# A gated encoder layer: the first column pair's ramp products made plainly, one matmul at a time

## The chip, the cores and the metric

The kernel runs on one core of a Trainium2 chip. The metric is device time in microseconds of one execution. The core's engines appear in the profile as PE (TensorE matmuls) and PEld (TensorE weight loads), DVE (VectorE), ACT (ScalarE), POOL (GpSimd) and SP (SyncE, which issues nearly all loads and stores).

## The reference

One encoder layer on x of 1024 tokens by 2048 channels, all in float32:

```python
mod = jax.nn.silu(c) @ w_ada + b_ada                    # w_ada is 2048 x 6144
shift, scale, gate = jnp.split(mod, 3, axis=-1)
h = rmsnorm(x, pre_g) * (1.0 + scale[:, None]) + shift[:, None]
proj = h @ w_in                                          # 2048 x 4608
q, k, v, gate_a, u, gate_p = jnp.split(proj, SPLIT_POINTS, axis=-1)
y_a = windowed_gqa(q, k, v, rel_table, sink) * jax.nn.silu(gate_a)
y_p = multiscale_pool(u, w_pool_grp, pool_scale) * jax.nn.silu(gate_p)
g = jax.nn.sigmoid(h @ w_merge + b_merge)                # 2048 x 4096
g_a, g_p = jnp.split(g, N_BRANCHES, axis=-1)
merged = g_a * (y_a @ w_br_attn) + g_p * (y_p @ w_br_pool)
o = merged @ w_out
return x + gate[:, None] * rmsnorm(o, post_g)
```

## The kernel before

**The big product.** h times the 8704 columns of w_in and w_merge is worked in 34 column pairs of 256 columns, in the order of the list `ORDER`. Its contraction over 2048 channels is done in two passes of 1024 channels, that is, eight row tiles of 128 (`PART[0]`, then `PART[1]`); the sums of the first pass go to DRAM and are added in the second. A pass of a pair is one call of `strassen`: seven products in place of eight blocks. The operands on h's side are seven combinations, `MOVING = ("B11", "T3", "T2", "B21", "T4", "T1", "B22")`, each made once for a pair of row tiles, "tile j" below (j = 0 to 3 for the first pass, tile j being channel tiles 2j and 2j+1), of 128 x 512 elements. The operands on the weights' side are made anew for every column pair.

Each float32 operand is split by `split` (L93) into a high part (ScalarE copies to fp32r, L95) and a low part (VectorE subtracts, L96). A product is three matmuls for each tile j: high by high, high by low, low by high (L235). With two tiles a pair takes 7 x 2 x 3 = 42 matmuls, with four 84.

**The ramp.** No product can start before x is normalised, turned (transposed by TensorE against a scaled identity, `turn_rows`, L407), and modulated by scale and shift, and these come from silu(c) times w_ada, 256 columns per tile j. `modulation(j, ...)` is four steps of four w_ada tiles each: a TensorE matmul per w_ada tile (`GEMV`, L455; two records each in the trace), then in the last step a copy of the sums (L462), sums over columns (`PM`, L426), and two small VectorE operations that write `modc` (L430, L433). `fill(j)` then modulates the four xT blocks of tile j in place (two on ScalarE at L502, two on VectorE at L504), forms the combinations, and splits all seven (`put`).

To start before all of w_ada is there, the first `RAMP = 4` column pairs are done in halves: first with tiles 0 and 1 alone, results to `ramp_d`, then with tiles 2 and 3, adding those parts (`ramp_gen`). Modulations 2 and 3 stand as side steps between the products of the first half (`side`, called from `run`), `fill(2)` and `fill(3)` after it. The first pair's first three weights are prepared early (`ahead=True`). `run` leaves each pair's last product to the next pair (`flush`). After the ramp, 22 pairs carry one list of side work in the first pass, and the remaining pairs carry another (the second half of x and its modulation, 38 steps).

**Buffers and order.** All instructions are written by a Python program and put in order, for each engine, by a planner that takes the program's order as priority and may move a ready instruction ahead of one that isn't ready. `keep` pins an instruction to its place in the program among those that are pinned. 56 shared buffers of 256 KB (`slot`) hold xT, rows of x, w_ada tiles and in the end the 4 x 14 operands; a load waits until its buffer is free. `claim(j)` reserves tile j's 14. PSUM has eight banks under the tags `mm` (2), `sc` (2), `at` (2), `z0` and `z1` (`SEEDED`). `OPEN` is one matmul in each seeded bank ahead of its first accumulation (L578).

Of the kernel before, what the change touches and what calls it, by code (L numbers as in the profile page):

```python
# [3 lines left out]

# [8 lines left out]
F32 = mybir.dt.float32  # L13
F32R = mybir.dt.float32r
AF = mybir.ActivationFunctionType
ALU = mybir.AluOpType
# [26 lines left out]
def encoder_layer(ctx: ExitStack, tc: tile.TileContext, x, c, table, w_ada, b_ada, pre_g,  # L43
# [32 lines left out]
    def uid(s):  # L76
        cnt[0] += 1
        return f"{s}_{cnt[0]}"
# [42 lines left out]

    NIN = 4608
    JP = KT // 4
    RAMP = 4
    bias_d = dram.tile([NH, P * LINE], F32, name="bias_d")
    line_d = dram.tile([NH, LINE], F32, name="line_d")
    part_d = dram.tile([NIN + 2 * D, S], F32, name="part_d")
# [49 lines left out]
            fill()  # L177
        fills.extend([fill] * len(groups))

    def load_raws(w, n0, rows, js):  # L180

        raws = []
        nj = len(js)
        joint = wp.tile([P, 2, nj, 256], F32, tag="raw", name=uid("raw"), bufs=4) if nj < 4 else None
        for kh in range(2):
            r = joint[:, kh] if nj < 4 else wp.tile([P, nj, 256], F32, tag="raw", name=uid("raw"), bufs=4)
            load(r, rows(w, js, kh)[:, :, n0:n0 + 256])
            raws.append(r)
        return raws

# [16 lines left out]
            load(parts[blk], part(blk))  # L207
        return parts

    def strassen(w, n0, rows, js, op, ev, finish, part=None, raws=None, ahead=False):  # L210

# [55 lines left out]
        if ahead:  # L267
            wts = iter(list(wts))
            yield
# [88 lines left out]

    scz = xa2.tile([P, KT, 32], F32, name="scz")
    nc.vector.memset(scz, 0.0)  # L360
    pr = bank("at")
    nc.tensor.transpose(pr[:, 0:104], rows, ident[0:104, 0:104])
    nc.scalar.activation(sc, pr[:, 0:16], AF.Silu)
    nc.scalar.activation(scz[:, :, 0], pr[:, 0:16], AF.Silu)
    nc.scalar.activation(cols, pr[:, 0:104], AF.Copy)

    PART = [range(8), range(8, 16)]
    xT = {}
# [15 lines left out]
    def norm_rows(si):  # L384
        ssq = ep.tile([P, 8], F32, tag="ssq", name=f"ssq{si}", bufs=4)
        for q in range(4):
            xt = xts[si, q]
            if q < 2:
                junk = bank("sc", "junk")
                nc.scalar.activation(junk, xt, AF.Square, accum_out=ssq[:, q:q + 1])  # L390
# [5 lines left out]
        nc.scalar.activation(ssq[:, 5:6], ssq[:, 4:5], AF.Sqrt, bias=eps_t, scale=1.0 / D)  # L396
# [4 lines left out]
    def turn_rows(s):  # L401

        for q in range(2):
            banks = [bank(t, "XT1") for t in ("mm", "mm", *SEEDED)]
            for m in range(4):
                for j in range(4):
                    nc.tensor.matmul(banks[j][:, m * P:(m + 1) * P], xts[4 * s + m, q][:, j * P:(j + 1) * P],  # L407
                                     turn[4 * s + m], start=True, stop=True)
            for j in range(4):
                if j % 2 == 0:  # L410
                    nc.vector.tensor_copy(xT[q * 4 + j, s], banks[j])
                else:
                    nc.scalar.activation(xT[q * 4 + j, s], banks[j], AF.Copy)

    def ada_tile(j, q):
        at = xa.tile([P, 2, 4, P], F32, tag="xa", name=uid("ada"))
        for kk in range(2):
            r0 = (2 * q + kk) * P
            load(at[:, kk].rearrange("p (g h) n -> p g (h n)", g=2), w_ada[r0:r0 + P, 0:2 * D].rearrange("p (g n) -> p g n", g=2)
                 [:, :, j * 256:(j + 1) * 256])  # L420
        return at

    def sum_columns(acc):
# [5 lines left out]
    def mod_columns(j, pm):  # L429
        tc.keep_in_program_order(nc.vector.tensor_tensor(  # L430
            modc[:, :, :, j], pm[:, 0:4].rearrange("p (g h) -> p g h", g=2),
            cols[:, 16:48].rearrange("p (g k) -> p g k", g=2)[:, :, 2 * j:2 * j + 2], ALU.add))
        nc.vector.scalar_tensor_tensor(modc[:, 1, :, j], modc[:, 1, :, j], 1.0,  # L433
                                       cols[:, 48 + 2 * j:50 + 2 * j], op0=ALU.add, op1=ALU.mult)

    def ada_slots(j):
        tiles = []
        for kc in range(KT):
            tiles.append(slot("ada", F32, (P, 4, P)))
            load(tiles[kc].rearrange("p (g h) n -> p g (h n)", g=2),  # L440
                 w_ada[kc * P:(kc + 1) * P, 0:2 * D].rearrange("p (g n) -> p g n", g=2)
                 [:, :, j * 256:(j + 1) * 256])
        return tiles

    def modulation(j, tile_of, pin=False):

        st_ = {}

        def step(q):
            if q == 0:  # L450
                st_["pv"] = bank("at", "GEMV")
            pv = st_["pv"]
            for kc in range(4 * q, 4 * q + 4):
                g = kc % 4 * 32
                ins = nc.tensor.matmul(pv[g:g + 32, :], scz[:, kc, :], tile_of(kc), start=kc < 4,  # L455
                                       stop=kc >= 12, tile_position=(0, g))
                if pin:
                    tc.keep_in_program_order(ins)
            if q == 3:
                acc = xa2.tile([P, 4, P], F32, tag="acc", name=uid("acc"), bufs=2)  # L460
                tc.keep_in_program_order(
                    nc.scalar.activation(acc, pv.rearrange("p (g n) -> p g n", g=4), AF.Copy))  # L462
                mod_columns(j, sum_columns(acc))

        return [lambda q=q: step(q) for q in range(4)]

    def weigh(acc, t, kc):

# [27 lines left out]

        return [(lambda q=q: load_(q), lambda q=q: sum_(q)) for q in range(8)], lambda: mod_columns(j, st_["pm"])

    def modulate(eng, t, k):
        j, kh = k // 2, k % 2  # L500
        if eng is nc.scalar:
            eng.activation(t, t, AF.Identity, scale=modc[:, 1, kh, j:j + 1], bias=modc[:, 0, kh, j:j + 1])  # L502
        else:
            eng.tensor_scalar(t, t, modc[:, 1, kh, j:j + 1], modc[:, 0, kh, j:j + 1],  # L504
                              op0=ALU.mult, op1=ALU.add)

    op = new_op()
    PAIRS = (NIN + 2 * D) // 256
# [10 lines left out]
    def fill(j):  # L519
# [13 lines left out]
        for name, src in (("T3", b11), ("T4", b21), ("T1", b12), ("B22", b22)):  # L533
            put(op, name, j, src)

    def ramp_gen(jj, i, parts, **kw):
# [6 lines left out]
    raws = [load_raws(*weight_of(ORDER[0]), rows_in_turn(0), [0, 1])]  # L543
    ada = [ada_slots(0), ada_slots(1)]
    claim(0)
    ada.append(ada_slots(2))
    claim(1)
    raws += [load_raws(*weight_of(ORDER[i]), rows_in_turn(0), [0, 1]) for i in range(1, RAMP)]
    ada3 = [ada_tile(3, q) for q in range(5)]

    def tile3(kc):
        if kc // 2 == len(ada3):
            ada3.append(ada_tile(3, kc // 2))
        return ada3[kc // 2][:, kc % 2]

    side = deque(modulation(2, ada[2].__getitem__, True))
    for n, step in zip((6, 9, 12, 15), modulation(3, tile3, True)):
        side.extend([lambda: None] * (n - len(side)) + [step])
    for s in range(2):
        for si in range(4 * s, 4 * s + 4):  # L560
            norm_rows(si)
        turn_rows(s)
    early.close()
    nc.vector.tensor_scalar(nsink_t, sink_t, -1.0, None, op0=ALU.mult)
    for step in modulation(0, ada[0].__getitem__):
        step()
    fill(0)
    gen = ramp_gen(0, 0, None, ahead=True)
    next(gen)
    for step in modulation(1, ada[1].__getitem__):  # L570
        step()
    fill(1)

    for tag in SEEDED:
        hi = op["B11"][0][0]
        nc.tensor.matmul(bank(tag, "OPEN"), hi[:, 0:P], hi, start=True, stop=True)  # L578
# [885 lines left out]
```

## Time and profile before

| what | value |
|---|---|
| median of 3 runs | 2123.35 us (2121.32 to 2123.44) |
| profiled execution, its own time | 2122.46 us |
| its span | 2120.7 us, 28959 instructions |
| mean granted TensorE clock | 0.998 |
| HBM traffic | 340.41 MB read, 125.85 MB written |

The page gives busy time by engine, the span in 40 slices, and the chain of waits that ended last. A row of the timeline has start, duration, engine, line, operation, result and operands, the count, and in brackets the idle time before it and what ended it. A row of the windows has the stretch, its length, the busy time of PE, PEld, DVE, ACT and POOL with the number of instructions, the granted TensorE clock (1.00 is full), the DMA share and GB/s; when asked for one line only, the engines that this line runs on. A row of the chain has start, duration and what the chain ran through. Matmuls are pipelined, so the duration of one is longer than its spacing from the next.

### The profile page before, as it was taken

To read this page: it belongs to the slowest core of one execution; us is meant where nothing else is said; L and a number is where in the kernel's file an instruction comes from. 1 tells how busy PE (TensorE), PEld (TensorE's weight loads), DVE (VectorE), ACT (ScalarE), POOL (GpSimd) and SP (SyncE) were. 2 spreads that over 40 slices of the span, in tenths; PEclk is the share of its full clock that TensorE was granted. 3 is DMA by queue.
4 is the path that set the end of the run, shared out by engine and by line. 5 is a ranking of instruction groups with operands and counts; after the bars stand their busy time and mean duration, and the time that the engine had idled before them with its cause. 6 is when DMAs were issued, how large, how long until landed. Compare 5 with 4: busy or idle time off the path is not lost.

```text
span 2120.7 us, 28959 instructions
## 1 busy us (share of the span) xinstructions
PE 2089.0 (99%) x9567; PEld 1715.1 (81%) x9567; DVE 1538.7 (73%) x2754; ACT 1109.5 (52%) x2102; POOL 20.4 (1%) x90
## 2 busy tenths in 40 slices
PE   6999999999999999999999999999999999999998
PEld 4588888888888888888888888888788788888886
DVE  5786667777547676677777678856957977889667
ACT  5654444444474544666665544333645644767654
POOL 0000000000000000000000000000000000000000
PEclk9999999999999999999999999999999999999999
DMA  9886566899676356544645477676754556686996
GB/s 330 271 269 216 187 208 219 307 310 316 223 228 210 120 176 204 174 157 159 196 149 162 154 236 235 206 221 195 237 173 160 187 194 198 218 311 216 296 342 221
DMA packets 301718, 466.10 MB, mean 220 GB/s; under 512 B 23882, under 2 KB 144866, under 8 KB 301568
## 3 DMA queue, kind: packets, MB, share of 16 engines
q1 hardware_dynamic: 298192, 455.72, 65.9%
q0 software_dynamic: 3040, 8.48, 1.1%
q8 instruction: 75, 1.23, 0.2%
q14 instruction: 75, 0.61, 0.1%
q10 hardware_dynamic: 336, 0.06, 0.0%
HBM read 340.41 MB, written 125.85 MB: 220 GB/s over the span
## 4 chain that ended last, share of the span: by engine, by line
PE 90%; DVE 5%; DMA 3%; issue 1%; ACT 1%; SPq 0%; ACTq 0%; DVEq 0%
PE Z L235 30%; PE X L235 20%; PE V L235 20%; PE Z L1194 2%; PE Z L1195 2%; PE Z L1196 2%; PE V L1196 1%; PE X L1196 1%; PE X L1195 1%; PE V L1195 1%; PE V L1194 1%; PE X L1194 1%; PE GEMV L455 1%; DMA raw<-in_w_merge_dram 1%; DVE wlo L96 1%; PE PT L905 1%
## 5 line engine op out<-in xcount | busy, mean ns | idle before, releaser
L95 ACT ACTIVATE whi<-raw 128x512 fp32r<-128x512 f32 (+1 forms) x528 | 321.8, 610 | 526.1 <-PE Z L235 260.4
L96 DVE TENSOR_TENSOR wlo<-raw,whi 128x512 fp32r<-128x512 f32 (+1 forms) x528 | 347.0, 661 | 166.7 <-PE Z L235 129.8
L96 DVE TENSOR_TENSOR wlo<-wr,whi 128x512 fp32r<-128x512 f32 x224 | 151.0, 688 | 55.9 <-ACT whi L95 49.8
L95 ACT ACTIVATE whi<-wr 128x512 fp32r<-128x512 f32 x224 | 138.8, 629 | 89.7 <-DVE wlo L96 37.2
L102 DVE TENSOR_TENSOR raw<-raw,raw 128x512 f32<-128x512 f32 x80 | 55.2, 690 | 105.0 <-DMA raw<-in_w_merge_dram 77.2
L235 PE MATMUL V<-T3h,whi 128*128 128x512 f32 x336 | 92.0, 393 | 0.6 <-DVE u L102 0.6
L235 PE MATMUL X<-B11h,whi 128*128 128x512 f32 x336 | 92.0, 392 | 0.0
L95 ACT ACTIVATE whi<-ws 128x512 fp32r<-128x512 f32 (+1 forms) x88 | 53.7, 611 | 73.0 <-PE X L235 67.7
L235 PE MATMUL V<-T4l,whi 128*128 128x512 f32 x336 | 91.2, 390 | 0.7 <-DVE T4l L96 0.6
L235 PE MATMUL Z<-T1h,whi 128*128 128x512 f32 x336 | 91.6, 391 | 0.0
L235 PE MATMUL Z<-T2h,whi 128*128 128x512 f32 x336 | 91.5, 392 | 0.1
L235 PE MATMUL Z<-B22h,whi 128*128 128x512 f32 x336 | 91.5, 392 | 0.0
L235 PE MATMUL Z<-T2h,wlo 128*128 128x512 f32 x336 | 90.8, 390 | 0.5 <-DVE wlo L96 0.5
L235 PE MATMUL X<-B21h,whi 128*128 128x512 f32 x336 | 91.2, 391 | 0.0
L235 PE MATMUL V<-T4h,whi 128*128 128x512 f32 x336 | 91.2, 391 | 0.0
L235 PE MATMUL Z<-T1l,whi 128*128 128x512 f32 x336 | 91.0, 390 | 0.1
L235 PE MATMUL X<-B11l,whi 128*128 128x512 f32 x336 | 90.9, 390 | 0.0
L235 PE MATMUL X<-B11h,wlo 128*128 128x512 f32 x336 | 90.7, 390 | 0.0
L235 PE MATMUL Z<-B22l,whi 128*128 128x512 f32 x336 | 90.7, 390 | 0.0
L235 PE MATMUL V<-T3l,whi 128*128 128x512 f32 x336 | 90.7, 390 | 0.0
L235 PE MATMUL Z<-T1h,wlo 128*128 128x512 f32 x336 | 90.6, 390 | 0.0
L235 PE MATMUL X<-B21l,whi 128*128 128x512 f32 x336 | 90.6, 389 | 0.0
(315 smaller groups left out, 4819.3 us busy)
## 6 DMA issues: line engine op xcount, KB each, us to landing
part<-part_d SPq DMA_DIRECT2D x136, 256.0 KB, 4.8
ada<-in_w_ada_dram SPq DMA_DIRECT2D x128, 256.0 KB, 5.3
raw<-in_w_in_dram SPq DMA_DIRECT2D x64, 512.0 KB, 4.1
raw<-in_w_merge_dram SPq DMA_DIRECT2D x64, 512.0 KB, 5.8
wr<-ws_dS SPq DMA_DIRECT2D x64, 512.0 KB, 5.2
wr<-in_w_out_dram SPq DMA_DIRECT2D x48, 512.0 KB, 5.4
proj_d<-part SPq DMA_DIRECT2D x68, 256.0 KB, 2.2
sw<-in_w_out_dram SPq DMA_DIRECT2D x64, 256.0 KB, 5.7
```

What stands on the lines that cost most here:

```text
L95: ins = (nc.scalar.activation(hi, src, AF.Copy), nc.vector.tensor_tensor(lo, src, f32(hi), ALU.subtract))
L96: nc.vector.tensor_tensor(lo, src, f32(hi), ALU.subtract))
L102: return (eng or nc.vector).tensor_tensor(o, a, b, ALU.add)
L235: nc.tensor.matmul(ps, w_[:, i], op[mov][j][m_], start=fresh and i == 0 and n == 0, stop=i == nj - 1 and n == 2, skip_group_check=True)
L455: ins = nc.tensor.matmul(pv[g:g + 32, :], scz[:, kc, :], tile_of(kc), start=kc < 4, stop=kc >= 12, tile_position=(0, g))
L905: nc.tensor.transpose(pt[:, i * P:(i + 1) * P], p[:, i * P:(i + 1) * P], ident)
L1194: nc.tensor.matmul(pb, hi, w[0], start=first, stop=False, skip_group_check=True)
L1195: nc.tensor.matmul(pb, lo, w[0], start=False, stop=False, skip_group_check=True)
L1196: nc.tensor.matmul(pb, hi, w[1], start=False, stop=last, skip_group_check=True)
```

## The change

- The first column pair's first half is no longer a `strassen` call. `plain_block` makes each of its four result blocks from 12 matmuls (48 for 42), `piece` by `piece`, all pinned, in `mm` banks for the left half of tokens and `sc` banks for the right. Its weights are the raw ones, split (`first_weights(j)`).
- The pieces of tile 0 stand between the `GEMV` matmuls of modulation 1, tile 1's after it. The last round of x transposes (`turn_round`) stands between those of modulation 0, in two half rounds.
- `fill(0)` and `fill(1)` become `fill_blocks`, in which ScalarE writes the high part of each modulated block directly while VectorE modulates in place and subtracts, and `fill_sums` for the combinations. The upper right block gets operands of its own (`B12h`, `B12l`) in a pool that is freed after the plain products.
- The second ramp pair's first two weights are split ahead and given to it (`given`).
- `RAMP` is 5. Loads of w_ada for group 3 go partly to shared buffers (six of 16), and the raw weight loads are spread: pair 0's after group 0, pairs 1 and 2 after group 1, pairs 3 and 4 after group 3. Raw loads and the `ada_tile` loads are pinned.
- Modulation 2's first step stands before the last plain block; its other steps and those of modulation 3 stand at every second side slot of the next two pairs.
- Small vectors' activations follow the first row tile's squares.

```diff
-    RAMP = 4
+    RAMP = 5
...
-            yield prep(a11)
-            s3 = wp.tile([P, nj, P], F32, tag="ws", name=uid("ws"))
-            sub(s3, a11, a21)
-            yield prep(s3)
+            yield from given
+            if not given:
+                yield prep(a11)
+                s3 = wp.tile([P, nj, P], F32, tag="ws", name=uid("ws"))
+                sub(s3, a11, a21)
+                yield prep(s3)
...
+    def fill_blocks(j, between=None):
+        (b11, b12), (b21, b22) = ((xT[k, 0], xT[k, 1]) for k in (2 * j, 2 * j + 1))
+        right = tuple(bp.tile([P, 512], F32R, tag=t, name=uid(t)) for t in ("B12h", "B12l"))
+        for n, ((hi, lo), t, k) in enumerate(((op["B11"][j], b11, 2 * j), (op["B21"][j], b21, 2 * j + 1),
+                                              (right, b12, 2 * j), (op["B22"][j], b22, 2 * j + 1))):
+            keep(modulate(nc.scalar, t, k, hi))
+            keep(modulate(nc.vector, t, k))
+            if n < 3:
+                keep(sub(lo, t, f32(hi)))
+            if between:
+                between(n)
+        return right
+
+    def fill_sums(j):
+        (b11, b12), (b21, b22) = ((xT[k, 0], xT[k, 1]) for k in (2 * j, 2 * j + 1))
+        keep(sub(b12, b12, b11))
+        t2 = rp.tile([P, 512], F32, tag="tf", name=uid("tf"), bufs=2)
+        keep(sub(t2, b22, b12))
+        keep(sub(b11, t2, b11))
+        hi, lo = op["B22"][j]
+        keep(sub(lo, b22, f32(hi)))
+        split(*op["T3"][j], b11, True)
+        split(*op["T2"][j], t2, True)
+        keep(sub(b21, b21, t2))
+        for name, src in (("T4", b21), ("T1", b12)):
+            split(*op[name][j], src, True)
...
+    ada = [ada_slots(0)]
+    fetch_raws(0)
+    ada.append(ada_slots(1))
+    fetch_raws(1)
+    fetch_raws(2)
     claim(0)
     ada.append(ada_slots(2))
     claim(1)
     ada3 = [ada_tile(3, q) for q in range(5)]
+    ada3 = [at[:, kk] for at in ada3 for kk in range(2)] + ada_slots(3, range(10, KT))
+    for i in range(3, RAMP):
+        fetch_raws(i)
+    group2 = deque(modulation(2, ada[2].__getitem__, True))
+    side = deque()
+    for n, step in zip((1, 3, 5, 7, 9, 11, 13), list(group2)[1:] + modulation(3, ada3.__getitem__, True)):
+        side.extend([lambda: None] * (n - len(side)) + [step])
...
+    def plain_block(blk, j):
+        nt, s = int(blk[0]) - 1, int(blk[1]) - 1
+        def piece(n):
+            if j == n == 0:
+                opened[blk] = bank("mm" if s == 0 else "sc", "PB")
+            whi, wlo = (w[:, :, nt * P:(nt + 1) * P] for w in weights0[j])
+            mov = (op["B11"][j], op["B21"][j]) if s == 0 else (right_top[j], op["B22"][j])
+            kh, w, m = ((0, whi, 0), (0, wlo, 0), (1, whi, 0), (1, wlo, 0), (0, whi, 1), (1, whi, 1))[n]
+            keep(nc.tensor.matmul(opened[blk], w[:, kh], mov[kh][m], start=j == n == 0,
+                                  stop=j == 1 and n == 5, skip_group_check=True))
+            if j == 1 and n == 5:
+                t = ev.tile([P, 512], F32, tag="ev", name=uid("c"))
+                keep(nc.scalar.activation(t, opened[blk], AF.Copy))
+                store(block(ramp_d[0], 0)(blk), t)
+        return [partial(piece, n) for n in range(6)]
...
+    s0, s1, s2, s3 = modulation(0, ada[0].__getitem__, True)
+    turns, put_by = turn_round(1, 1, (0, 1))
+    s0()
+    s1()
+    take(turns, 8)
+    put_by()
+    turns, put_by = turn_round(1, 1, (2, 3))
+    s2()
...
+    s3(while_copied, lambda: take(turns, 1))
+    take(turns, 3)
     early.close()
...
+    right_top.append(fill_blocks(0))
+    put_by()
+    first_weights(1)
+    s0, s1, s2, s3 = modulation(1, ada[1].__getitem__, True)
+    pieces = deque(p for blk in ("11", "21", "12", "22") for p in plain_block(blk, 0))
+    take(pieces, 6)
+    s0()
+    take(pieces, 6)
+    s1()
+    fill_sums(0)
+    s2(None, lambda: take(pieces, 1))
...
+    s3(while_copied, lambda: take(pieces, 1))
+    take(pieces, 2)
+    right_top.append(fill_blocks(1, lambda n: n == 1 and split(second["hi"][1], second["lo"][1], second["s3"], True)))
+    fill_sums(1)
+    pieces = deque(p for blk in ("11", "21", "12", "22") for p in plain_block(blk, 1))
+    take(pieces, 18)
+    group2.popleft()()
+    take(pieces, 6)
+    second = ramp_gen(0, 1, None, given=list(zip(second["hi"], second["lo"])))
...
-    for _ in range(2):
-        side.popleft()()
     parts = {}
-    for i in range(RAMP):
-        run(ramp_gen(0, i, None) if i else gen, side, range(7),
+    for i in range(1, RAMP):
+        run(second if i == 1 else ramp_gen(0, i, None), side, range(7),
```

More of the change, by code (lines that the diff above doesn't have):

```diff
@@ L2 @@
 from collections import deque
+from functools import partial
 from contextlib import ExitStack
@@ L178, in fill_op, with load_raws @@
         fills.extend([fill] * len(groups))
-    def load_raws(w, n0, rows, js):
+    def load_raws(w, n0, rows, js, pin=False):
         raws = []
@@ L186, in load_raws @@
             r = joint[:, kh] if nj < 4 else wp.tile([P, nj, 256], F32, tag="raw", name=uid("raw"), bufs=4)
-            load(r, rows(w, js, kh)[:, :, n0:n0 + 256])
+            ins = load(r, rows(w, js, kh)[:, :, n0:n0 + 256])
+            if pin:
+                keep(ins)
             raws.append(r)
@@ L208, in load_parts, with strassen @@
         return parts
-    def strassen(w, n0, rows, js, op, ev, finish, part=None, raws=None, ahead=False):
+    def strassen(w, n0, rows, js, op, ev, finish, part=None, raws=None, given=()):
         nj = len(js)
@@ L399, in norm_rows, with turn_round, turn_one, put_by @@
         nc.vector.tensor_scalar(turn[si], ident, rstd[:, si:si + 1], None, op0=ALU.mult)
-    def turn_rows(s):
-        for q in range(2):
+    def turn_round(s, q, js):
+        banks = [bank(t, "XT1") for t in SEEDED]
+        def turn_one(m, n):
+            keep(nc.tensor.matmul(banks[n][:, m * P:(m + 1) * P], xts[4 * s + m, q][:, js[n] * P:(js[n] + 1) * P],
+                                  turn[4 * s + m], start=True, stop=True))
+        def put_by():
+            keep(nc.vector.tensor_copy(xT[q * 4 + js[0], s], banks[0]))
+            keep(nc.scalar.activation(xT[q * 4 + js[1], s], banks[1], AF.Copy))
+        return deque(partial(turn_one, m, n) for m in range(4) for n in range(2)), put_by
+    def turn_rows(s, qs):
+        for q in qs:
             banks = [bank(t, "XT1") for t in ("mm", "mm", *SEEDED)]
@@ L418, in ada_tile @@
             r0 = (2 * q + kk) * P
-            load(at[:, kk].rearrange("p (g h) n -> p g (h n)", g=2), w_ada[r0:r0 + P, 0:2 * D].rearrange("p (g n) -> p g n", g=2)
-                 [:, :, j * 256:(j + 1) * 256])
+            keep(load(at[:, kk].rearrange("p (g h) n -> p g (h n)", g=2),
+                      w_ada[r0:r0 + P, 0:2 * D].rearrange("p (g n) -> p g n", g=2)[:, :, j * 256:(j + 1) * 256]))
         return at
@@ L432, in mod_columns, with ada_slots @@
             cols[:, 16:48].rearrange("p (g k) -> p g k", g=2)[:, :, 2 * j:2 * j + 2], ALU.add))
-        nc.vector.scalar_tensor_tensor(modc[:, 1, :, j], modc[:, 1, :, j], 1.0,
-                                       cols[:, 48 + 2 * j:50 + 2 * j], op0=ALU.add, op1=ALU.mult)
-    def ada_slots(j):
+        keep(nc.vector.scalar_tensor_tensor(modc[:, 1, :, j], modc[:, 1, :, j], 1.0,
+                                            cols[:, 48 + 2 * j:50 + 2 * j], op0=ALU.add, op1=ALU.mult))
+    def ada_slots(j, kcs=range(KT)):
         tiles = []
-        for kc in range(KT):
+        for kc in kcs:
             tiles.append(slot("ada", F32, (P, 4, P)))
-            load(tiles[kc].rearrange("p (g h) n -> p g (h n)", g=2),
+            load(tiles[-1].rearrange("p (g h) n -> p g (h n)", g=2),
                  w_ada[kc * P:(kc + 1) * P, 0:2 * D].rearrange("p (g n) -> p g n", g=2)
@@ L447, in modulation, with step @@
         st_ = {}
-        def step(q):
+        def step(q, between=None, each=None):
             if q == 0:
@@ L458, in step @@
                     tc.keep_in_program_order(ins)
+                if each:
+                    each()
             if q == 3:
@@ L462, in step @@
                     nc.scalar.activation(acc, pv.rearrange("p (g n) -> p g n", g=4), AF.Copy))
+                if between:
+                    between()
                 mod_columns(j, sum_columns(acc))
-        return [lambda q=q: step(q) for q in range(4)]
+        return [partial(step, q) for q in range(4)]
     def weigh(acc, t, kc):
@@ L542, in encoder_layer, with fetch_raws @@
     fetch_rows_of_x(1)
-    raws = [load_raws(*weight_of(ORDER[0]), rows_in_turn(0), [0, 1])]
-    ada = [ada_slots(0), ada_slots(1)]
+    raws = []
+    def fetch_raws(i):
+        raws.append(load_raws(*weight_of(ORDER[i]), rows_in_turn(0), [0, 1], True))
+    ada = [ada_slots(0)]
[3 more added lines that the diff above has]
+    fetch_raws(2)
     claim(0)
@@ L561, in encoder_layer, with first_weights @@
             norm_rows(si)
-        turn_rows(s)
-    early.close()
[L564 to L572, printed above, removed]
+        turn_rows(s, range(2 - s))
+    keep(nc.vector.tensor_scalar(nsink_t, sink_t, -1.0, None, op0=ALU.mult))
+    weights0 = []
+    def first_weights(j):
+        hi, lo = (wp.tile([P, 2, 256], F32R, tag=t, name=uid(t), bufs=4) for t in ("whi", "wlo"))
+        for kh in range(2):
+            split(hi[:, kh], lo[:, kh], raws[0][kh][:, j], True)
+        weights0.append((hi, lo))
@@ new lines, in take, with while_copied @@
+    def take(queue, n):
+        for _ in range(min(n, len(queue))):
+            queue.popleft()()
+    s0, s1, s2, s3 = modulation(0, ada[0].__getitem__, True)
[6 more added lines that the diff above has]
+    s2()
+    def while_copied():
+        first_weights(0)
+        take(turns, 1)
+    s3(while_copied, lambda: take(turns, 1))
+    take(turns, 3)
+    early.close()
+    bp = held.enter_context(pool("b12", side="right"))
@@ new lines, in encoder_layer, with while_copied @@
+    right_top.append(fill_blocks(0))
[9 more added lines that the diff above has]
+    s2(None, lambda: take(pieces, 1))
+    second = {}
+    def while_copied():
+        take(pieces, 2)
+        (a11, a21), second["hi"], second["lo"] = (raws[1][0][:, :, nt * P:(nt + 1) * P] for nt in range(2)), [], []
+        for n in range(2):
+            second["hi"].append(wp.tile([P, 2, P], F32R, tag="whi", name=uid("whi"), bufs=4))
+            second["lo"].append(wp.tile([P, 2, P], F32R, tag="wlo", name=uid("wlo"), bufs=4))
+        split(second["hi"][0], second["lo"][0], a11, True)
+        second["s3"] = wp.tile([P, 2, P], F32, tag="ws", name=uid("ws"))
+        keep(sub(second["s3"], a11, a21))
@@ L576, in encoder_layer @@
+    s3(while_copied, lambda: take(pieces, 1))
+    take(pieces, 2)
+    assert not pieces
+    right_top.append(fill_blocks(1, lambda n: n == 1 and split(second["hi"][1], second["lo"][1], second["s3"], True)))
[5 more added lines that the diff above has]
+    second = ramp_gen(0, 1, None, given=list(zip(second["hi"], second["lo"])))
     for tag in SEEDED:
         hi = op["B11"][0][0]
-        nc.tensor.matmul(bank(tag, "OPEN"), hi[:, 0:P], hi, start=True, stop=True)
```

43 lines of the change are left out of this document (22 added, 21 removed).

## The prediction

> **What bounds the kernel now.** I read the page first: shares, slices, chain.
>
> ```profile
> PE 2089.0 (99%) x9567; PEld 1715.1 (81%) x9567; DVE 1538.7 (73%) x2754; ACT 1109.5 (52%) x2102; POOL 20.4 (1%) x90
> PE   6999999999999999999999999999999999999998
> PE 90%; DVE 5%; DMA 3%; issue 1%; ACT 1%; SPq 0%; ACTq 0%; DVEq 0%
> ```
>
> TensorE is full except in the first slice (53 us) and a little at the end; 90% of the chain is its matmuls. So only the ramp can give time, or a shorter TensorE programme, and the change makes that six matmuls longer. But a busy TensorE in the ramp is not a useful one. The windows over all instructions and over the product line (L235) alone show it:
>
> ```profile
> 50.00:60.00 10.00, 9.71 (x40) 2.98 (x38) 5.62 (x12) 3.41 (x6) 0.85 (x9) 1.00 1.10 349
> 60.00:70.00 10.00, 10.00 (x46) 4.40 (x44) 8.53 (x16) 7.42 (x15) 0.00 (x0) 1.00 1.10 348
> 54.40:93.85 39.45, 21.93 (x84) 15.26 (x85) 1.00 0.97 309
> 93.85:113.90 20.05, 20.05 (x90) 16.55 (x89) 1.00 0.52 170
> ```
>
> By 93.85 us 84 product matmuls are done; from there products run without a gap, and whatever the ramp wins there goes to the end undiminished. 84 products are two pairs' first halves (42 each) and would fill 19 us; they took 39.5, with the DMA saturated at 348 GB/s. The timeline of TensorE and the chain in order of time say what stood between:
>
> ```profile
> 37.27 3.84 PE L407 MATMUL XT<-turn,xt 128*128 128x128 f32 x32
> 45.35 1.05 PE L426 MATMUL PM<-ones,acc 128*128 128x1 f32 x8 [0.69 <-ACT acc L462]
> 46.33 8.27 PE L455 MATMUL GEMV<-ada,scz 128*32 128x512 f32 x28
> 54.53 0.72 PE L578 MATMUL OPEN<-B11h 128*128 128x512 f32 x2
> 57.20 1.05 PE L426 MATMUL PM<-ones,acc 128*128 128x1 f32 x8 [0.29 <-ACT acc L462]
> 58.18 3.88 PE L455 MATMUL GEMV<-ada,scz 128*32 128x512 f32 x16
> 72.40 3.21 PE L455 MATMUL GEMV<-ada,scz 128*32 128x512 f32 x8 [0.47 <-DMA ada<-in_w_ada_dram]
> 79.87 1.07 PE L455 MATMUL GEMV<-ada,scz 128*32 128x512 f32 x8
> 80.86 0.73 PE L235 MATMUL V<-T3h,whi 128*128 128x512 f32 x2
> 92.51 0.94 PE L426 MATMUL PM<-ones,acc 128*128 128x1 f32 x8
> 93.32 0.72 PE L235 MATMUL X<-B11h,wlo 128*128 128x512 f32 x2
> ```
>
> ```profile
> 66.25 6.02 DMA ada<-in_w_ada_dram
> 102.24 1.36 PE X L235 x6
> ```
>
> Products cost 1.36/6 = 0.227 us each. A step of four w_ada tiles is 8 records and 1.0 us (79.87 to 80.86); the column sums add 0.8 (92.51 to 93.32). Between 46.3 and 54.5 TensorE only follows w_ada tiles as they land, and no product can run although tile 0's operands are being made; at 72 it waits for group 3. That waiting room is what the change wants to fill.
>
> **The loads.** The queue of SP:
>
> ```profile
> 25.10 36.31 SPq L440 DMA_DIRECT2D ada<-in_w_ada_dram  x48
> 61.73 4.15 SPq L187 DMA_DIRECT2D raw<-in_w_in_dram  x6
> 66.25 7.16 SPq L419 DMA_DIRECT2D ada<-in_w_ada_dram  x10
> 80.38 2.48 SPq L419 DMA_DIRECT2D ada<-in_w_ada_dram  x5
> 85.37 0.43 SPq L419 DMA_DIRECT2D ada<-in_w_ada_dram  x1
> ```
>
> A 256 KB load takes 0.75 us at 348 GB/s. The first of the ten loads of group 3, the 89th load in order, lands at 66.25 + 6.02 = 72.3; counting back, the 66th (x, first raws, groups 0 and 1) lands near 55. In the new order the same 66 stand ahead of group 1's end. Four raw loads now stand ahead of group 2, whose last (the 86th) lands at about 70; I reckon its last step at 78, so this is hidden for 8 us. Group 3's last six tiles go to the 56 shared buffers: 12 of xT, 28 claimed operands and 16 of group 2 fill them, so these loads wait for two steps of group 2 (67 and 73 us), and land 6 us later, near 79, where before the last six were issued at 80 to 86. TensorE gets to them at 90. On SP only the fourth and fifth pairs' raws stand behind this wait, wanted near 96. Cost nothing.
>
> **The operands of tile 0.** Rows of VectorE and ScalarE:
>
> ```profile
> 40.48 1.29 DVE L411 COPY xT<-XT 128x512 f32<-128x512 f32 x2 [3.13 <-PE XT L407]
> 44.70 0.60 ACT L462 ACTIVATE acc<-GEMV 128x512 f32<-128x512 f32 x1 [2.85 <-PE GEMV L455]
> 46.84 1.52 ACT L502 ACTIVATE xT<-xT,modc 128x512 f32<-128x512 f32 x2 [1.54 <-DVE modc L433]
> 59.30 1.00 DVE L504 TENSOR_SCALAR xT<-xT,modc 128x512 f32<-128x512 f32 x2
> 61.54 0.68 DVE L96 TENSOR_TENSOR B11l<-xT,B11h 128x512 fp32r<-128x512 f32 x1
> 66.36 0.68 DVE L96 TENSOR_TENSOR B22l<-xT,B22h 128x512 fp32r<-128x512 f32 x1
> 66.96 0.75 DVE L96 TENSOR_TENSOR wlo<-raw,whi 128x256 fp32r<-128x256 f32 x2
> 93.49 0.17 DVE L430 TENSOR_TENSOR modc<-PM,cols 128x4 f32<-128x4 f32 x1 [1.58 <-PE PM L426]
> 98.11 0.69 DVE L96 TENSOR_TENSOR B11l<-xT,B11h 128x512 fp32r<-128x512 f32 x1 [0.51 <-ACT B11h L95]
> 107.82 0.68 DVE L96 TENSOR_TENSOR B22l<-xT,B22h 128x512 fp32r<-128x512 f32 x1
> ```
>
> The first modulation starts at 46.84, 2.14 after the copy of the sums (44.70). The 32 records of the last round of transposes are 16 transposes at 0.24; four of them now come after group 0's last GEMV or between, so the copy comes about 1.0 earlier and tile 0's fill starts at 45.8. From there VectorE is in a fixed order. Prices: a subtraction 0.60 (eight from 61.54 to 66.36), a modulation 0.50, a ScalarE modulation 0.76, a PSUM copy 0.65, a weight low part 0.35. `fill_blocks`: 0.8 for the first ScalarE part, 4 x 0.5 + 3 x 0.6, together 4.6. Then the put-by copy 0.65, two weight parts 0.7, `fill_sums` 9 x 0.6 = 5.4, the second pair's low part and difference 0.7. Sum 12.1: 57.9. On TensorE's side group 1 ends near 55.5, a piece later 55.75, plus 2.14: 57.9 too. Both come together; with the two small column operations the second modulation starts at 58.1, against 59.30. TensorE meanwhile needs 24 pieces x 0.227 = 5.4 and 16 tiles (4.0) in the 11 us after 46.6: the first tile's half of pair 0 is hidden completely.
>
> **From 58.1 to the dense stretch.** `fill_blocks` 4.6, the second weight part between 0.35, three subtractions 1.8, B22's low part 0.7: at 65.6 the last operand of block 12 is there. Then a piece 0.23, group 2's first step 1.0, block 22's six pieces 1.36, two OPEN matmuls 0.66 (the 54.53 row, less its overlapped tail): pair 1 starts at 68.85. Pairs 1 and 2 up to group 3's end: 78 products, 17.7; seven steps 7.0; two column sums 1.6. That is 95.15, with 120 products' worth done: pair 0 counts as the 42 it replaces, its 48 being paid already. Before, at 95.15, 84 + 1.27/0.227 = 89.6 were done. 30.4 products x 0.227 = **6.9 us gained**.
>
> **The fifth ramp pair.** Its 84 products are the same in two halves. What it adds (four stores, four loads, VectorE's additions) lies beside dense TensorE work, as in the 93.85 to 113.9 row, where DMA is at 0.52. It is needed as cover: tile 3's operands took from 93.49 to 108.5, 15 us after the sums, while 84 products (19 us) were left, a margin of 4. Now 90 are left (20.4 us): a margin of 5. Without this pair the margin would be negative and most of the gain would go back. The second pass over the other rows has a pair less for its side work: its 38 steps need 6.3 of 7 pairs.
>
> **Unknown prices.** The trace has no product alternating with single GEMVs: between nothing and 0.1 us each (the change of kind at 80.86 costs 0.1), eight times: at most 0.8, mostly under the DMA wait; I take 0. The pair 1 product X isn't pinned and could slip into TensorE's 1.5 us wait for B22: from 0 to -1.4; I take 0. Raws of pairs 1 and 2 landing ahead of group 1 would cost 4 x 0.75 = 3.0; I take 0, since the unpinned raws of before kept their place behind 48 w_ada loads.
>
> TensorE's clock could fall in the thinner stretch at 58 to 66:
>
> ```profile
> 28.00:30.00 2.00, 0.79 (x7) 0.60 (x6) 1.93 (x8) 1.89 (x7) 0.20 (x2) 1.00 1.09 355
> 32.00:34.00 2.00, 2.00 (x9) 1.10 (x7) 1.87 (x9) 0.34 (x2) 0.29 (x3) 0.51 1.10 348
> 34.00:36.00 2.00, 2.00 (x9) 1.01 (x8) 1.15 (x4) 0.68 (x2) 0.10 (x1) 0.63 1.10 347
> 44.00:47.00 3.00, 2.31 (x18) 1.23 (x17) 0.49 (x3) 0.76 (x2) 0.00 (x0) 1.00 1.11 349
> ```
>
> After a stretch at 40% busy it was granted 0.51 and 0.63, (0.49 + 0.37) x 2 = 1.7 us lost; after one at 77% it kept 1.00. I reckon 6.4 us of work in the 10 from 58.1, nearer to the second: between 0 and 1.7, taken as 0. The Trainium skill, "TensorE: Matmul & The Clock Gate", Part 1, states that about 3.4 us of idleness halve the clock and as long at work restores it; the dip in this trace agrees in depth (0.51), though TensorE wasn't idle that long before it. By that rule the new stretch stays at full clock, its longest wait being 1.5 us; by the row it could cost the 1.7.
>
> **Rivals.**
> A, forecast: gain 6.9; own range from 5 to 8.3.
> B, partial: the fixed order lets something stand in front: raws ahead of group 1 (3.0), alone or with the clock (1.7). Gain 2.2 to 3.9, times 2119.4 to 2121.1. For it: pinned orders have little slack here, two chains meeting at 57.9. Against: the DMA order above.
> C, nothing: group 3's sums or tile 3's fill come over 5 us later than reckoned, so the ramp's second half waits for operands and takes the gain back: about 2123. Against: two steps per pair, and the margin above.
> D, slower: the pinned ScalarE-VectorE alternation. On the way from 45.8 to B22 there are some 17 hand-overs that I price at nothing. At 6.9/17 = 0.4 us each the gain is gone; at 0.7 each it is 11.9 - 6.9 = 5 us slower, about 2128.4. For it: VectorE idled 0.51 for ScalarE at 98.11. Against: from 61.54 to 66.36 eight such operations ran without a gap.
> That the change doesn't do what it says (the planner puts other work before the pieces) falls under B.
>
> **How the numbers follow.** The profiled execution took 2122.46 us for a span of 2120.7; 2122.46 - 6.9 = 2115.6. The median of the runs, 2123.35, is 0.9 above the profiled one, so the forecast is 2116.4. Chances: A 0.68, B 0.14, C 0.05, D 0.13. What a measurement can tell here is 0.2%, 4.25 us, so A is faster, B and C the same, D slower. A alone spans 2115.0 to 2118.3, and a little more for the run-to-run spread; the range reaches from 2112.5 over A, B and half of C to 2123.0, and leaves out D.
>
> **What would show it.** Product matmuls between 47 and 57 us; the second modulation at about 58; pair 1's X at 67 to 69; group 3's column sums near 95 with dense products after; tile 3's B22 low part before 115. Wrong if the second modulation starts after 61, if a wait for w_ada or an operand stands in front of products after 70, if the clock falls below 0.9 between 58 and 72, or if gaps appear where the ramp's second half begins, near 116.

## The result and the profile after

The changed kernel takes 2131.39 us (median of 6 runs, 2129.11 to 2136.23), the kernel before 2122.82 us (6 runs). The ratio is 1.0043, 95% interval 1.003 to 1.0056: slower by some 9 us, where 2116.4 was forecast. The profiled execution took 2130.61 us for a span of 2128.8, 8.1 longer than before.

The page of the changed kernel, the lines that answer to the three of before:

```profile
PE 2095.2 (98%) x9573; PEld 1716.0 (81%) x9573; DVE 1542.5 (72%) x2768; ACT 1108.2 (52%) x2105; POOL 20.0 (1%) x90
PE   6999999999999999999999999999999999999998
PE 91%; DMA 5%; DVE 3%; issue 1%; ACT 1%; SPq 0%; ACTq 0%; DVEq 0%
```

At this height nothing has moved: six matmuls more, the first slice as thin as before. The windows show where the time is. The first three rows are over all instructions, the last two over the product line (now L238):

```profile
50.00:60.00 10.00, 10.00 (x35) 2.98 (x34) 7.98 (x14) 2.30 (x4) 0.87 (x11) 0.85 1.10 349
60.00:70.00 10.00, 9.01 (x30) 3.52 (x29) 2.71 (x8) 2.82 (x6) 0.30 (x3) 1.00 1.10 348
70.00:80.00 10.00, 9.54 (x32) 5.86 (x30) 9.10 (x18) 3.97 (x8) 0.00 (x0) 0.66 1.02 324
54.40:93.85 39.45, 9.93 (x38) 6.94 (x39) 0.91 0.93 298
110.12:130.00 19.88, 19.88 (x89) 16.45 (x88) 1.00 0.51 155
```

TensorE is again "busy" throughout and again not usefully so: 35 and 30 instructions in 10 us, where dense products make 45. In the stretch in which the kernel before did 84 products, 38 are done beside the plain pieces; the gapless stretch begins at 110.12. By then pair 0 (worth 42) and 84 products are done, 126; the kernel before had done 84 + (110.12 - 93.88)/0.227 = 155.5. The ramp has lost 29.5 x 0.227 = 6.7 us of the 8.1. The timeline of TensorE shows how:

```profile
55.74 0.50 PE L647 MATMUL PB<-B12h,whi 128*128 128x512 f32 x1
56.17 1.05 PE L479 MATMUL GEMV<-ada,scz 128*32 128x512 f32 x2
57.15 0.50 PE L647 MATMUL PB<-B12h,wlo 128*128 128x512 f32 x1
57.57 1.04 PE L479 MATMUL GEMV<-ada,scz 128*32 128x512 f32 x2
...
77.26 1.06 PE L479 MATMUL GEMV<-ada,scz 128*32 128x512 f32 x8
...
80.49 0.73 PE L238 MATMUL X<-B11h,whi 128*128 128x512 f32 x2
```

One w_ada tile (two records) takes 1.05 us when a product stands on either side. Four of them side by side take 1.06 (77.26). A tile and a piece come every 1.40 us (56.17, 57.57), and eight such pairs make 11.2 us where the forecast had 3.8: 2.0 for eight tiles and 1.8 for eight pieces. ScalarE's rows give the two modulations, and the copies of the plain blocks out of PSUM (`c`):

```profile
45.86 0.81 ACT L530 ACTIVATE B11h<-xT,modc 128x512 fp32r<-128x512 f32 x1 [0.98 <-issue]
68.08 0.81 ACT L530 ACTIVATE B11h<-xT,modc 128x512 fp32r<-128x512 f32 x1 [1.50 <-issue]
...
79.34 0.62 ACT L96 ACTIVATE T1h<-xT 128x512 fp32r<-128x512 f32 x1
79.86 2.04 ACT L651 ACTIVATE c<-PB 128x512 f32<-128x512 f32 x4
```

The first modulation starts at 45.86 as forecast (45.8), the second at 68.08 against 58.1, and pair 1's first product at 80.49 against 68.85.

### The profile page after: what moved, and what is told of

It reads as the page before. It is cut to its first block, busy times and chain, and to the rows that moved or that the text cites. A ratio compares the mean times of both kernels' runs of the same rounds, so it can differ in the third digit from the quotient of the medians.

```text
span 2128.8 us, 29011 instructions
## 1 busy us (share of the span) xinstructions
PE 2095.2 (98%) x9573; PEld 1716.0 (81%) x9573; DVE 1542.5 (72%) x2768; ACT 1108.2 (52%) x2105; POOL 20.0 (1%) x90
## 4 chain that ended last, share of the span: by engine, by line
PE 91%; DMA 5%; DVE 3%; issue 1%; ACT 1%; SPq 0%; ACTq 0%; DVEq 0%
PE Z L238 31%; PE X L238 20%; PE V L238 20%; DMA ada<-in_w_ada_dram 2%; PE Z L1325 2%; PE Z L1326 2%; PE Z L1327 2%; PE X L1326 1%; PE V L1327 1%; PE X L1327 1%; PE V L1326 1%; PE X L1325 1%; PE V L1325 1%; DMA xt<-in_x_dram 1%; PE PT L1036 1%; DVE wlo L97 1%
## 5 line engine op out<-in xcount | busy, mean ns | idle before, releaser
L238 PE MATMUL Z<-T1h,whi 128*128 128x512 f32 x334 | 91.5, 392 | 0.3 <-ACT u L248 0.3
L238 PE MATMUL X<-B11h,whi 128*128 128x512 f32 x334 | 91.4, 392 | 0.1
L238 PE MATMUL Z<-T2h,whi 128*128 128x512 f32 x334 | 91.1, 392 | 0.4 <-ACT whi L96 0.4
L238 PE MATMUL V<-T3h,whi 128*128 128x512 f32 x334 | 91.2, 392 | 0.2 <-DVE u L103 0.2
L238 PE MATMUL Z<-T2h,wlo 128*128 128x512 f32 x334 | 90.3, 390 | 0.9 <-DVE wlo L97 0.9
L238 PE MATMUL Z<-B22h,whi 128*128 128x512 f32 x334 | 91.1, 392 | 0.0
L238 PE MATMUL X<-B21h,whi 128*128 128x512 f32 x334 | 90.8, 391 | 0.0
L238 PE MATMUL V<-T4h,whi 128*128 128x512 f32 x334 | 90.7, 391 | 0.0
L238 PE MATMUL V<-T4l,whi 128*128 128x512 f32 x334 | 90.5, 390 | 0.1
L238 PE MATMUL Z<-T1l,whi 128*128 128x512 f32 x334 | 90.4, 390 | 0.1
L238 PE MATMUL X<-B11l,whi 128*128 128x512 f32 x334 | 90.4, 390 | 0.0
L238 PE MATMUL Z<-T1h,wlo 128*128 128x512 f32 x334 | 90.3, 390 | 0.0
L238 PE MATMUL X<-B11h,wlo 128*128 128x512 f32 x334 | 90.2, 390 | 0.0
L238 PE MATMUL Z<-B22l,whi 128*128 128x512 f32 x334 | 90.2, 390 | 0.0
L238 PE MATMUL V<-T3l,whi 128*128 128x512 f32 x334 | 90.2, 390 | 0.0
L238 PE MATMUL X<-B21l,whi 128*128 128x512 f32 x334 | 90.2, 390 | 0.0
```

The source lines that it names most:

```text
L238: nc.tensor.matmul(ps, w_[:, i], op[mov][j][m_], start=fresh and i == 0 and n == 0, stop=i == nj - 1 and n == 2, skip_group_check=True)
```

## The experiments

Theory T: the four w_ada matmuls of a step each use 32 columns of the array and run side by side as long as they are neighbours in TensorE's queue; a full-width product between them ends that. Rivals: K, the half clock (0.66 in the 70 to 80 row); R, the fifth ramp pair and the later loads. All variants are edits of the changed kernel; the kernel before was timed beside them (medians 2122.89 for runs 1 to 4, 2123.54 for 5 to 8 and 2123.47 for 9 to 12), and each ratio is to it.

**1. Group 1 whole.**

```diff
-    s2(None, lambda: take(pieces, 1))
+    s2()
+    take(pieces, 8)
...
-    s3(while_copied, lambda: take(pieces, 1))
+    s3(while_copied)
```

> Group 1's steps are taken whole: eight pieces stand between its third and fourth step instead of one behind each of the eight w_ada matmuls. Theory T (the four w_ada matmuls of a step run side by side in TensorE's column groups, 1.0 us for four, and a product between them makes each take its 1.0 us alone): the stretch of 8 x 1.40 = 11.2 us shrinks to about 2 x 1.2 + 8 x 0.23 = 4.3, the second modulation moves from 68.1 to 60 or 61, the kernel comes to 2131.4 - 7.5 = about 2124. Rival K (the half-clock stretches at 50 and at 70 to 77 us cost the time): the order of eight matmuls changes little, 2130 to 2131. Rival R (the fifth ramp pair and the later load of group 2 cost it): no change, 2131.

2124.76 us, ratio 1.0009 (0.9999 to 1.0018). The second modulation moved from 68.08 to 62.02 (60 to 61 expected), though the first came 1.7 later than in the changed kernel. The clock fell here too (0.51 and 0.50 from 64 to 70), and the fifth pair and the loads are as they were: K and R are out as main causes. T's time (about 2124) was met.

**2 and 3. Group 0 whole; both whole.**

```diff
-    s3(while_copied, lambda: take(turns, 1))
+    take(turns, 4)
+    s3(while_copied)
```

> Group 0's last step is taken whole: the four transposes stand ahead of it instead of one behind each w_ada matmul; group 1 is as in the changed kernel. Theory T: four alternations of 1.40 become 1.2 + 4 x 0.24 = 2.2, 3.4 us less, so the first modulation moves from 45.9 to between 42.5 and 44; group 1's tiles then hold the next steps back (they land until 54.5), so the second modulation gains only 0 to 2 us: 2129.5 to 2131.4. Rivals K and R: no change.

> Both groups' steps are taken whole. Theory T: the second modulation at 57.5 to 60, pair 1's first product near 70, the kernel at 2121 to 2124, so at or a little under the kernel before. Rivals K and R: 2130 to 2131.

Group 0 alone: 2130.17 us, ratio 1.0031 (1.0021 to 1.0041); first modulation at 44.63 (42.5 to 44 expected), second at 65.31, so it gained 2.8 where at most 2 were expected. These rows are of the fastest of its eight executions, 2125.96, with the clock at 1.00 from 40 to 67. Both: 2121.59 us, ratio 0.9992 (0.9984 to 1.0001). ScalarE's and TensorE's rows of the kernel with both groups whole:

```profile
59.31 0.81 ACT L530 ACTIVATE B11h<-xT,modc 128x512 fp32r<-128x512 f32 x1 [1.50 <-issue]
```

```profile
51.34 1.92 PE L479 MATMUL GEMV<-ada,scz 128*32 128x512 f32 x16
...
55.26 1.06 PE L479 MATMUL GEMV<-ada,scz 128*32 128x512 f32 x8
...
68.07 0.50 PE L647 MATMUL PB<-B22l,whi 128*128 128x512 f32 x1 [1.42 <-DVE B22l L106]
...
71.72 0.73 PE L238 MATMUL X<-B11h,whi 128*128 128x512 f32 x2
```

The second modulation is 8.8 us earlier than in the changed kernel, and so is pair 1's first product. The whole loss is gone, but not much is won.

**4. Dose: pieces behind every second w_ada matmul of group 1.**

```diff
-    s2(None, lambda: take(pieces, 1))
+    s2(None, lambda kc: kc % 2 and take(pieces, 2))
```

(and the same in `s3`)

> Dose: in group 1's third and fourth step two pieces stand behind every second w_ada matmul. Theory T: two w_ada matmuls still run side by side, so a step takes 2 x (1.0 + 0.2 + 2 x 0.23) = 3.3 us instead of 5.6; the second modulation comes 4.6 us earlier, at 63.5, and the kernel at about 2127, between the changed kernel and the one with whole steps. If the cost were one of switching per change of kind (four changes fewer of 16), the gain would be half of that of whole steps as well; what tells them apart is the duration of a pair of w_ada matmuls in the trace: 1.0 us for two under T, under 0.6 for two if only the switch costs.

```profile
54.63 1.91 PE L479 MATMUL GEMV<-ada,scz 128*32 128x512 f32 x12
...
57.12 1.05 PE L479 MATMUL GEMV<-ada,scz 128*32 128x512 f32 x4
58.10 0.50 PE L647 MATMUL PB<-B22h,whi 128*128 128x512 f32 x1
58.44 0.40 PE L647 MATMUL PB<-B22h,wlo 128*128 128x512 f32 x1
58.77 1.05 PE L479 MATMUL GEMV<-ada,scz 128*32 128x512 f32 x4
```

Two tiles take 1.05 us, as one does and as four do. A fixed price for each change of kind would look the same, but six neighbours (the first row) take 1.91 and eight (run 3, the 51.34 row) 1.92: the time goes by groups of up to four tiles, so it is the side-by-side running that is lost. Second modulation at 64.06 (63.5 expected), 2126.37 us, ratio 1.0013 (1.0004 to 1.0022). From the first modulation to the second it is 22.2 us in the changed kernel, 20.7 in run 2 with the same order in group 1, 15.9 here, and 14.5 in runs 1 and 3.

This run also settles K for the stretch behind the second modulation. Windows of it, and then of the changed kernel, after the second modulation:

```profile
64.00:67.00 3.00, 1.86 (x5) 0.78 (x5) 2.26 (x5) 2.94 (x5) 0.00 (x0) 1.00 1.11 349
70.00:73.00 3.00, 0.78 (x4) 0.35 (x2) 2.91 (x7) 0.81 (x2) 0.00 (x0) 1.00 1.11 349
```

```profile
68.00:71.00 3.00, 2.06 (x5) 0.88 (x5) 2.26 (x5) 2.92 (x5) 0.00 (x0) 0.83 1.11 349
71.00:74.00 3.00, 2.54 (x7) 1.95 (x7) 3.00 (x7) 0.62 (x2) 0.00 (x0) 0.50 1.10 348
74.00:77.00 3.00, 3.00 (x9) 2.02 (x7) 2.90 (x7) 0.79 (x2) 0.00 (x0) 0.53 1.10 348
```

With the clock at 1.00 pair 1's first product came at 76.47, 12.41 us after the modulation (64.06); at half clock it was 80.49 - 68.08 = 12.41 as well. The slow pieces there cost nothing: something else set the 12.4.

**5. What sets the 12.4: B22's low part first, tile 0's T4 and T1 later.** This run and all that follow have whole steps in both groups, as run 3. The line `keep(sub(lo, b22, f32(hi)))` moves to the head of `fill_sums`, and both tiles' T4 and T1 are split after `fill_sums(1)`.

> On top of whole steps in both groups: B22's low part stands first among the sums, and the two operands T4 and T1 of tile 0 are split after tile 1's sums. With whole steps TensorE waits 1.42 us for B22's low part, and the copy of group 1's sums starts 0.66 us after its last w_ada matmul, behind T4 and T1 on ScalarE. Theory (VectorE's and ScalarE's fixed order sets the way from one modulation to the next and to pair 1): both waits go, second modulation at 58.6 instead of 59.3, pair 1's first product 11.0 us after it instead of 12.4, the kernel 2 us faster than with whole steps alone, about 2119.5. Rival K (the half-clock stretch after the second modulation sets that way): no more than 0.7 faster, 2121.

```profile
69.10 0.63 PE L715 MATMUL OPEN<-B11h 128*128 128x512 f32 x2
71.50 0.73 PE L238 MATMUL X<-B11h,whi 128*128 128x512 f32 x2 [1.77 <-ACT c L650]
...
72.80 1.05 PE L238 MATMUL X<-B11h,wlo 128*128 128x512 f32 x2
```

2123.86 us, ratio 1.0002 (0.9993 to 1.0011): a miss, 2119.5 was expected. Both waits went, and a third stood behind them. Pair 1's products want the two `mm` banks of blocks 11 and 21, whose copies are pinned on ScalarE behind T4 and T1, here those of both tiles. TensorE now idled 1.77 us, and the half clock fell on pair 1's own products (1.05 for two instead of 0.62), where it does cost.

**6, 7, 8. Four ramp pairs; joined steps; B22 first and joined together.** The first is `RAMP = 4`; in the second, steps of groups 2 and 3 stand in twos.

> Whole steps in both groups, with four ramp pairs as before the change. The claim of the prediction (the fifth pair is needed as cover, since tile 3's operands take 15 us after its sums and 9.5 us of products would be left): the second half waits some 5 us, 2126 to 2127. Rival (the products want the operands one after the other, 1.36 us apart, and T3, the second, would be ready 11.5 us after the sums when it is wanted at 11.4): at most 1 us, so 2121 to 2122.5, the same as with five.

> Whole steps in both groups, and the steps of groups 2 and 3 joined in twos: two ahead of the last plain block, then three pairs of steps between products. If a step costs its 1.0 us and 0.23 for the product behind it that starts afresh (chain: 1.59 us instead of 1.36), and two joined steps take 1.92 as in group 1, four joins save about 0.3 each: 1.2 us, 2120.4. If a step's price is 1.0 us alone, as in the prediction's sum, joining saves 4 x 0.1 at most: 2121.2.

> Whole steps, B22's low part first, T4 and T1 of tile 0 later, and joined steps together. If the three costs lie one after the other on TensorE's way they add up: 2121.6 - 2.0 - 1.2 = about 2118.4, a ratio of 0.998 to the kernel before. If the loads of groups 2 and 3 come to bind, at least 1 us of that is missing.

Four pairs: 2121.51 us, ratio 0.9996 (0.9987 to 1.0004), like five. The fifth pair wasn't needed; TensorE's waits show 0.7 us for T4's low part. Joined: 2122.3, 0.9991 (0.9982 to 0.9999). The first full pair after the ramp starts at 165.32 instead of 166.69, more than the 1.2 expected, but the kernel's 2120.4 wasn't reached. In the profiled execution (2124.22) a later wait stands against the gain:

```profile
PE b L908 <- ACT h L911: 2.7, 1, 2.7
```

That is an x transpose of the later side work waiting for a PSUM bank. Together: 2122.73, 0.9995 (0.9986 to 1.0004), no sum of the parts (2118.4 expected): T4, T1 and the copies stood in pair 1's way there as well, where its first product waited 1.67 us for a copy.

**9 and 10. The copies unpinned**, with B22 first; in 10 with tile 0's T4 and T1 later, so that it differs from 5 on ScalarE alone, but for a few small VectorE operations.

```diff
-                keep(nc.scalar.activation(t, opened[blk], AF.Copy))
+                nc.scalar.activation(t, opened[blk], AF.Copy)
```

> Whole steps, B22's low part first, and the four copies of the plain blocks out of PSUM no longer pinned behind tile 1's T3, T2, T4 and T1 on ScalarE (T4 and T1 of tile 0 stay where they were). In the run with B22 first, OPEN began at 69.10 and pair 1's first product at 71.50, right after the first of these copies (chain: T1h, then c, then X, with 71.45 the copy's end). Theory Q (the pinned copies hold the two banks that pair 1's products want): the product follows OPEN at once, at about 11.3 us after the second modulation instead of 12.4 with whole steps alone and 13.1 with B22 first; 2120.4, about 1.2 under whole steps alone. Rival (the low parts of the sums on VectorE hold pair 1 anyway): first product or the second (it wants T3) no earlier, 2121.6 or more.

> As the run with B22 first (T4 and T1 of tile 0 later too), with the copies of the plain blocks unpinned: the one difference from that run is ScalarE's order. Theory Q: the 2.0 us wait between OPEN and pair 1's first product goes, and with it the half-clock products behind it (2.36 and 2.25 us for six instead of 1.36): 1.5 to 3 us less than that run's 2123.9, 2121 to 2122; against whole steps alone 0 to 1 less. Rival: the wait stays, 2123 to 2124.

```profile
69.84 0.63 PE L715 MATMUL OPEN<-B11h 128*128 128x512 f32 x2
70.31 0.62 PE L238 MATMUL X<-B11h,whi 128*128 128x512 f32 x2
```

In 10 the product follows OPEN at once, 11.2 us after the second modulation (59.09): 2121.35 us, ratio 0.9992 (0.9984 to 1.0001), against 2123.86 in 5. In 9 (2121.42, 0.9992, 0.9983 to 1.0001) pair 1's first matmuls even slipped in ahead of block 12's last piece. Theory Q holds for the wait; the gain beside whole steps alone is not resolved.

**11 and 12. Together.**

> As the run with the copies free, and the steps of groups 2 and 3 joined in twos, which took the ramp's end from 166.7 to 165.3 us beside whole steps alone. If both gains stand one after the other, the ramp's end comes to 164.2 or less and the kernel to about 2119.2; if later waits in the order of side work take it back, as they did with joined steps alone (2.7 us in front of one x transpose), the ramp's end comes early and the kernel stays at 2121 to 2122.

> Everything together (whole steps, B22 first, T4 and T1 later, copies free, joined steps) with four ramp pairs. Four pairs cost nothing beside five with whole steps alone (2121.5 and 2121.6), though the second half then waited some 2 us for tile 3's operands. The earlier the first half runs ahead of group 3, the longer that wait: if it binds, the ramp's end comes to 146.5 again, no earlier than with whole steps and four pairs (146.7), 2121.5; if not, to 145 and the kernel to 2119 to 2120.

11: 2120.41 us, ratio 0.9987 (0.9978 to 0.9996), with the ramp's end at 164.66, between the two expectations. 12: 2118.61 us, ratio 0.9978 (0.9969 to 0.9987), faster than both kernels by a little; what four pairs and the later T4 and T1 give in it is not separated. Its first four-tile pair, and that of the kernel before (both with four ramp pairs):

```profile
145.09 1.07 PE L238 MATMUL X<-B11h,whi 128*128 128x512 f32 x4
```

```profile
149.68 1.07 PE L235 MATMUL X<-B11h,whi 128*128 128x512 f32 x4
```

The ramp ends 4.6 us earlier, and 4.0 of it arrive at the end of the span (2116.7).

## Why the prediction was wrong

Two of the prediction's own signs of being wrong showed: the second modulation came after 61, and the clock fell below 0.9 between 58 and 72.

**The ramp's start: right, with luck.** Tile 0's modulation came at 45.86 (45.8). With group 0's last step whole it came at 44.63 and 44.85 (runs 2 and 3), so single matmuls cost about 1 us here too; and in runs 1 and 4, with the same code up to there, it came at 47.56 and 48.13, with the clock at 0.50 from 31 to 34. Right as well: DMA saturated and never in TensorE's way after group 1, no gap where the second half begins.

**The unknown price of alternating: the step that failed.** "Between nothing and 0.1 us each" was read from the change of kind at 80.86, that is, from whole steps of eight records. Dividing 1.0 us by four gave 0.25 for a tile; alone it costs 1.05. The eight tiles so placed came to 11.2 us instead of 3.8. With whole steps the second modulation is at 59.31, not 68.08: 8.8 of the 10.0 us by which it was missed. Of these, 6.2 are group 1's order at full clock (20.7 against 14.5 us between the modulations), 1.0 is the earlier first modulation, and 1.5 are the half clock below. The trace of before had the price, a product, two tiles and a product:

```profile
55.10 0.40 PE L235 MATMUL X<-B11h,whi 128*128 128x512 f32 x1
55.42 1.05 PE L455 MATMUL GEMV<-ada,scz 128*32 128x512 f32 x4
56.41 0.50 PE L235 MATMUL V<-T3h,whi 128*128 128x512 f32 x1
```

Two tiles took 1.05 us there, as long as the four of a step. The Trainium skill, "TensorEngine Tiling (Array Packing)", Key Properties, states that different tiles of the array work in parallel and that a change of tiling mode drains TensorE; the changed kernel and run 4 agree with the first (1.05 for one or two tiles, 1.06 for four). Taken as a rival, eight tiles at 1.0 us each would have cost 8.0 in place of 2.0, an estimate of 2116.4 + 6.0 = 2122.4; the measured 11.2 makes it 2123.8.

**A step at 1.0 us: too small.** The product behind a step starts afresh. From the chain of waits of the changed kernel (start, duration, what):

```profile
82.15 1.36 PE V L238 x6
83.51 1.00 PE GEMV L479 x8
84.51 1.59 PE Z L238 x6
```

Six matmuls take 1.59 instead of 1.36. Seven steps and two column sums cost 2.0 us more than reckoned.

**From the second modulation to pair 1: 12.4 instead of 10.75.** Of the 1.65, 1.2 are VectorE's: in the changed kernel B22's low part ended 8.7 us after the modulation, where the sum had 7.5. Three weight operations that it hadn't priced, 0.34 us apart from what followed them, stood in front (the rows between are left out):

```profile
72.22 0.42 DVE L97 TENSOR_TENSOR wlo<-raw,whi 128x256 fp32r<-128x256 f32 x1
74.22 0.42 DVE L106 TENSOR_TENSOR ws<-raw 128x256 f32<-128x256 f32 x1
75.15 0.42 DVE L103 TENSOR_TENSOR raw<-raw 128x256 f32<-128x256 f32 x1
76.09 0.68 DVE L106 TENSOR_TENSOR B22l<-xT,B22h 128x512 fp32r<-128x512 f32 x1
```

The other 0.45 lie on TensorE, and some 0.27 of them in front of pair 1, whose first product came 0.74 us after OPEN against 0.47 in run 10. I also left out what was queued on ScalarE: copies pinned behind T4 and T1, with the banks of pair 1 behind them. In the changed kernel they ended at about the same time as TensorE's own work; they set the time once B22 came first (runs 5 and 10).

10.0 + 1.65 + 2.0 is 13.65, which is the way from -6.9 to +6.7 in the ramp.

**The fifth pair as cover: wrong.** I compared the time when all seven operands are there with the start of the second half; the products want them one by one (run 6).

**The clock: taken as nothing, and paid for elsewhere.** The fall to 0.50 at 70 to 76 cost nothing, but it had fallen earlier too, on group 1's tiles and pieces:

```profile
50.00:53.00 3.00, 3.00 (x12) 1.14 (x12) 2.96 (x7) 0.00 (x0) 0.17 (x2) 0.51 1.11 349
```

A step of group 1 took 1.94 us there (from 49.94) instead of 1.06. That is the 1.5 us between 22.2 and the 20.7 of run 2, where the clock stayed at 1.00. In run 5 it fell on pair 1's products, in run 10 on pieces in front of them (0.43 us apart instead of 0.23). Rival D had the right sign by another mechanism: beyond the three weight operations and what was priced, VectorE's way to B22 was some 0.2 us longer, all hand-overs together.

**Open:** 1.4 of the 8.1 us arise after the ramp. TensorE's waits after 118 us add up to 4.0 us, the longest 1.5, against 2.3 in the kernel before; no run isolates them.

## What to carry to other kernels

Before spreading work between small matmuls, ask whether they run side by side: the price of one is that of the group if it is the neighbourhood that makes it cheap, so fill between groups, never inside. Where an order is pinned, list for every engine what stands behind each pinned instruction, copies that free a PSUM bank first. Removing one wait shows the next: follow the chain until the engine runs dense.

## What the runs showed of the hardware

An fp32 w_ada tile on 32 columns took 1.05 us alone; two neighbours took as long, four 1.06, eight 1.92.

The half clock after a thin stretch does not follow from how thin it is: in run 4 TensorE was busy 1.86 of the 3 us from 64 and 0.78 of the 3 from 70 and kept 1.00, in the changed kernel it was busy 2.06 of the 3 us from 68, with the same code from there on, and fell to 0.50 (0.83 in that row, 0.50 in the next). The Trainium skill, "TensorE: Matmul & The Clock Gate", Part 1, has a free-running window of 3.4 us of idleness behind this; no wait of the changed kernel between the second modulation and the fall was longer than 1 us, so these rows don't agree with idleness of a whole window, while the dip's depth does.
